# Hybrid decoder block on one core: stores issued from GpSimd's queue in place of SyncE's

## The chip, the cores and the metric

The kernel runs on one core of one Trainium2 chip. The metric is device time in microseconds (us), the median of three runs: 1451.16 (1450.82 to 1451.53). The core's engines are TensorE (PE), VectorE (DVE), ScalarE (ACT), GpSimd (POOL) and SyncE (SP); each runs its own list of instructions in order, and semaphores order the lists against each other.

## The reference

One decoder block in fp32 over x of 1024 tokens and 1024 channels (D), with a feed-forward width of 2816. Norms and small steps are cut.

```python
h = rms_norm(x, norm_mix_g)
rnn_x, rnn_gate, sgu_u, sgu_v, gate_a, gate_b = split(h @ w_in)          # six of 1024 columns
rnn_x = causal_depthwise_conv(rnn_x, conv_w, conv_b)                     # width 4
y_a = gelu(rnn_gate) * rg_lru(rnn_x, ...)                                # gates, then a linear scan over time
y_b = chunked_sgu(gelu(sgu_u), gelu(sgu_v), ...)                         # u * (tril(W) LN(v) + b), chunks of 128
merged = sigmoid(gate_a) * (y_a @ w_proj_a) + sigmoid(gate_b) * (y_b @ w_proj_b)
x = x + merged @ w_out
h = rms_norm(x, norm_ffn_g)
g, u = split(h @ w_gate_up)
x = x + (silu(g) * u) @ w_down
return rms_norm(x, norm_final_g)
```

## The kernel before

Every fp32 operand of a large product is split into a high and a low part, and one product is three matmuls (L97 to L99): high by high, high by low, low by high. ACT makes the high part (L93), DVE the low part (L94). The matrix products run as Strassen-Winograd: a pair of output columns is seven products M1 to M7 on blocks and sums of blocks (`wino`), whose results DVE and ACT combine out of PSUM (L231 to L249: L236, L243 and L246 on DVE, L233, L239 and L241 on ACT). The order inside a pair is M1, M5, M6, M2, M7, M3, M4; some instructions end up in another place because the scheduler orders each engine's list.

The stages are: norm and transposes; SGU's v; then pairs of r (RG-LRU), u (SGU) and g (both merge gates) in the order of `IN`; projection b; projection a with the merge; output projection with residual; eleven pairs of the gated feed-forward; the down projection.

What one stage makes for a later one goes through DRAM. `store(dst, src)` (L724) writes it, `load` (L721) reads it back. `store` has five uses: `y_store` writes the blocks and block sums of the branch outputs to ya_d and yb_d (names of tiles: u_y, u_m, u_u, mix, yb_sd, yb_s for branch b, gg, ya_sd, ya_s for branch a); `gate_pair` writes the sigmoids to sga_d and sgb_d (tiles g_y, g_m, g_u, sg); `to_mb` writes projection b's gated result to mb_d (tiles pb_y, pb_m, pb_u, sb); `norm2` writes the residual to x2_d; `ff_outs` writes the feed-forward operands and their sums, made on GpSimd (L1147 to L1150), to ffa_d and ffs_d. All loads, the weights (wraw, L133) and the stores of the final output (L1240) are issued by SP as well, and SP does its instructions in order: a store whose data are not made yet holds what stands behind it.

The buffers that the text speaks of: ya_s and yb_s share two buffers (tag "s4"), written by DVE at L760 or in the sums below it; the staged loads (yb_r.., ya_r.., mrg, x2, ff) share the six buffers of `stg` (STG = 6); a gate of projection b is loaded one or two steps ahead into a tile sb. The program is built with `dynamic_dma_scratch_size=256` (L1350), the space in SBUF kept for descriptors of DMAs issued by GpSimd; the kernel before issues none.

Of the kernel before, what the change touches and what calls it, by code (L numbers as in the profile page):

```python
# [51 lines left out]
def block_kernel(ctx: ExitStack, tc: tile.TileContext, a: dict, out: bass.AP):  # L52
    nc = tc.nc
    act, dve, pool, pe = nc.scalar, nc.vector, nc.gpsimd, nc.tensor
# [667 lines left out]
        nc.sync.dma_start(dst, src)  # L722

    def store(dst, src):  # L724
        nc.sync.dma_start(dst, src)

    ms.__exit__(None, None, None)
    new_misc("misc1")
    with tc.tile_pool(name="phr", bufs=2) as wk:
# [12 lines left out]
        def y_store(d, name, f, h, y):  # L742


            k = f % 4
            n = "A12" if f >= 4 else "A11"
            if h == 0:
                store(d[n][:, k], y)
            elif f >= 4:
                store(d["A22"][:, k], y)  # L750
            else:
                store(d["sd"][:, k, 1], y)
            other = halves.pop((name, f, 1 - h), None)
            if other is None:
                halves[name, f, h] = y
                return
            y0, y1 = (y, other) if h == 0 else (other, y)
            s, r = halves.pop((name, f))
            if f < 4:
                dve.tensor_sub(s, y0, y1)  # L760
                store(d["sd"][:, k, 0], s)
                return
            dve.tensor_sub(r[:, 0], y1, r[:, 0])
            dve.tensor_add(r[:, 1], r[:, 1], y1)
            dve.tensor_sub(s, y0, r[:, 0])
            store(d["S2"][:, k], r[:, 0])
            store(d["S1"][:, k], r[:, 1])
            store(d["S4"][:, k], s)
# [591 lines left out]
```

## Time and profile before

| | |
|---|---|
| median of three runs | 1451.16 us (1450.82 to 1451.53) |
| profiled execution | 1452.88 us |
| its span, first to last instruction | 1451.2 us |
| granted TensorE clock, mean | 0.99 |
| busy: PE, DVE, ACT, POOL | 1400.2, 1098.3, 793.5, 74.8 us |

All durations come from the profiled execution. A line number is that of the kernel. In a time line each row is the start in us, the length in us, the engine, the line, the operation and what it writes and reads; a bracket at the end is the idle time of the engine ahead of it and what ended it. A DMA's row is its issue; when it has landed is a separate figure. PE's share of 96% means that what counts is where PE is not busy, and which other engine or transfer stands on the way at that moment.

### The profile page before, as it was taken

The numbers are of one execution on the slowest core, as the hardware profiler recorded it, in microseconds if no ns is written. First come the engines' busy times: TensorE is split into PE (matmuls) and PEld (weight loads), VectorE is DVE, ScalarE is ACT, GpSimd is POOL, SyncE is SP. The second block draws the span as 40 slices with busy tenths as digits, with TensorE's granted clock in tenths as the row PEclk, the third lists the DMA queues.
The fourth block names the chain that finished last, engine by engine and source line by source line (L and its number), as shares of the span: only waits on it lengthen the run. The fifth ranks groups of instructions, "written<-read, shape, count | busy, mean of one in ns | idle before, by whom it ended". The sixth has DMA issues, their size and how long they took to land.

```text
span 1451.2 us, 17181 instructions
## 1 busy us (share of the span) xinstructions
PE 1400.2 (96%) x6192; PEld 1153.3 (79%) x6192; DVE 1098.3 (76%) x1803; ACT 793.5 (55%) x1315; POOL 74.8 (5%) x59
## 2 busy tenths in 40 slices
PE   7998699999999999999999999999999999999997
PEld 5776587788888888778888788888888888888886
DVE  6878889988888878597855966666666665697585
ACT  6456668789888876262443633333333333444454
POOL 0000000000000000000000011111111111100000
PEclk9998899999999999999999999999999999999999
DMA  8412445632233367676531032222222226853342
GB/s 294 157 44 70 157 173 176 206 123 93 78 122 140 117 261 293 234 263 217 188 122 44 22 134 109 109 109 110 105 88 105 103 81 266 312 196 109 109 138 80
DMA packets 72821, 212.45 MB, mean 146 GB/s; under 512 B 6560, under 2 KB 20384, under 8 KB 60192
## 3 DMA queue, kind: packets, MB, share of 16 engines
q1 hardware_dynamic: 72592, 211.32, 40.8%
q8 instruction: 48, 0.79, 0.2%
q14 instruction: 37, 0.30, 0.1%
q10 hardware_dynamic: 144, 0.04, 0.0%
HBM read 148.68 MB, written 62.65 MB: 146 GB/s over the span
## 4 chain that ended last, share of the span: by engine, by line
PE 76%; DVE 11%; ACT 6%; DMA 4%; issue 2%; SPq 0%; DVEq 0%; ACTq 0%; POOL 0%; POOLq 0%
PE f_p L99 10%; PE f_p L97 10%; PE f_p L98 10%; PE d_M L98 5%; PE d_M L97 5%; PE d_M L99 5%; PE g_p L99 3%; PE g_p L98 3%; PE g_p L97 3%; PE r_p L99 2%; DMA sb<-sgb_d 2%; PE r_p L98 2%; PE r_p L97 2%; PE po L97 2%; PE po L99 2%; PE po L98 2%
## 5 line engine op out<-in xcount | busy, mean ns | idle before, releaser
L93 ACT ACTIVATE dl_M<-wraw 128x512 fp32r<-128x512 f32 x77 | 48.6, 631 | 104.8 <-PE d_M L99 89.8
L98 PE MATMUL d_M<-d_M,dl_M 128*128 128x512 f32 x264 | 102.8, 389 | 0.0
L97 PE MATMUL d_M<-d_M,dl_M 128*128 128x512 f32 x264 | 102.7, 389 | 0.0
L99 PE MATMUL d_M<-d_M,dl_M 128*128 128x512 f32 x264 | 102.7, 389 | 0.0
L93 ACT ACTIVATE f_t<-wraw 128x512 fp32r<-128x512 f32 x88 | 55.5, 630 | 83.8 <-PE f_p L99 71.4
L94 DVE TENSOR_TENSOR dl_M<-wraw,dl_M 128x512 fp32r<-128x512 f32 x77 | 54.0, 701 | 51.5 <-ACT dl_M L93 51.3
L94 DVE TENSOR_TENSOR f_t<-wraw,f_t 128x512 fp32r<-128x512 f32 x88 | 71.7, 815 | 23.7 <-ACT f_t L93 22.6
L97 PE MATMUL f_p<-m,f_b 128*128 128x512 f32 x176 | 69.2, 393 | 0.0
L98 PE MATMUL f_p<-m,f_b 128*128 128x512 f32 x176 | 69.0, 392 | 0.0
L99 PE MATMUL f_p<-m,f_b 128*128 128x512 f32 x176 | 69.0, 392 | 0.0
L98 PE MATMUL f_p<-m,f_t 128*128 128x512 f32 x176 | 68.5, 389 | 0.0
L99 PE MATMUL f_p<-f_S,f_t 128*128 128x512 f32 x176 | 68.5, 389 | 0.0
L97 PE MATMUL f_p<-f_S,f_t 128*128 128x512 f32 x176 | 68.5, 389 | 0.0
L99 PE MATMUL f_p<-m,f_t 128*128 128x512 f32 x176 | 68.5, 389 | 0.0
L97 PE MATMUL f_p<-m,f_t 128*128 128x512 f32 x176 | 68.5, 389 | 0.0
L98 PE MATMUL f_p<-f_S,f_t 128*128 128x512 f32 x176 | 68.5, 389 | 0.0
L93 ACT ACTIVATE f_b<-wraw 128x512 fp32r<-128x512 f32 x66 | 41.1, 626 | 36.8 <-PE f_p L99 31.6
L94 DVE TENSOR_TENSOR f_b<-wraw,f_b 128x512 fp32r<-128x512 f32 x66 | 45.3, 687 | 19.6 <-ACT f_b L93 18.9
L97 PE MATMUL pv<-wv,h 128*128 128x512 f32 x128 | 51.5, 403 | 7.8 <-ACT wv L93 7.8
L97 PEld LDWEIGHTS d_M<-d_M,dl_M 128*128 128x128 f32 x264 | 49.6, 188 | 10.4
L98 PEld LDWEIGHTS d_M<-d_M,dl_M 128*128 128x128 f32 x264 | 49.6, 188 | 10.3 <-DVE d_M L94 0.2
L99 PEld LDWEIGHTS d_M<-d_M,dl_M 128*128 128x128 f32 x264 | 49.6, 188 | 10.3
(504 smaller groups left out, 4213.0 us busy)
## 6 DMA issues: line engine op xcount, KB each, us to landing
wraw<-in_w_gu_dram SPq DMA_DIRECT2D x22, 1024.0 KB, 4.8
wd<-in_w_down_dram SPq DMA_DIRECT2D x11, 1024.0 KB, 9.4
wraw<-in_w_r_dram SPq DMA_DIRECT2D x8, 1024.0 KB, 6.1
wraw<-in_w_g_dram SPq DMA_DIRECT2D x8, 1024.0 KB, 4.8
wraw<-ffs_d SPq DMA_DIRECT2D x8, 1024.0 KB, 5.1
wraw<-ffa_d SPq DMA_DIRECT2D x6, 1024.0 KB, 6.1
xn<-in_x_dram SPq DMA_DIRECT2D x8, 512.0 KB, 6.2
wraw<-in_w_u_dram SPq DMA_DIRECT2D x4, 1024.0 KB, 5.3
```

Of the source, the lines that this page charges most:

```text
L93: act.activation(hi, src, AF.Copy)
L94: (eng or dve).tensor_sub(lo, src, hi.bitcast(F32))
L97: pe.matmul(o, lh, rh, start=start, stop=False, **kw)
L98: pe.matmul(o, lh, rl, start=False, stop=False, **kw)
L99: pe.matmul(o, ll, rh, start=False, stop=stop, **kw)
```

## The change

`store` issues its DMA from GpSimd (`pool`) in place of SP. Loads, weights, the spatial mix and the final output stay on SP.

```diff
--- before.py
+++ after.py
@@ -722,7 +722,7 @@
         nc.sync.dma_start(dst, src)
 
     def store(dst, src):
-        nc.sync.dma_start(dst, src)
+        pool.dma_start(dst, src)
 
     ms.__exit__(None, None, None)
     new_misc("misc1")
```

138 stores move. SP's list goes from 377 rows to 238, GpSimd's from 64 to 202. The other engines keep their work; some rows change places, because the scheduler sees other queues.

The first place is the burst of stores in which pair u2 ends while r0 makes its output. SP before (a load of mix and one of graw stand between the stores; the brackets name the semaphores that the row waits for, DMAHW those of DMAs from SP):

```order
L725 DMA yb_d_A_80<-u_y_1887 128x512 [waits DMAHW7_49,DVE_49]
L722 DMA mix_2060<-mix_d_108 128x512 [waits DMAHW4_49,DMAHW0_49]
L725 DMA yb_d_A_81<-u_m_1908 128x512 [waits DMAHW1_49,DVE_49]
L725 DMA ya_d_A_72<-gg_1723 128x512 [waits DMAHW2_49,DVE_49]
L725 DMA yb_d_S_83<-yb_sd_1996 128x512 [waits DMAHW3_49,DVE_49]
L725 DMA yb_d_S_82<-yb_sd_1996 128x512 [waits DVE_49]
L722 DMA graw_2074<-in_rg_w_dram 128x256 [waits DMAHW5_49,DVE_49]
L725 DMA yb_d_A_80<-u_u_1925 128x512 [waits DMAHW6_49,DVE_49]
L725 DMA yb_d_S_84<-yb_s_1995 128x512 [waits DMAHW7_49,DVE_49]
```

GpSimd after (DMASW are the semaphores of DMAs from GpSimd):

```order
L725 DMA yb_d_A_80<-u_y_1887 128x512 [waits DMASW4_49,DVE_49]
L725 DMA yb_d_A_81<-u_m_1908 128x512 [waits DMASW5_49,DVE_49]
L725 DMA ya_d_A_72<-gg_1723 128x512 [waits DMASW6_49,DVE_49]
L725 DMA yb_d_S_83<-yb_sd_1996 128x512 [waits DMAHW6_49,DMASW7_49,DVE_49]
L725 DMA yb_d_S_82<-yb_sd_1996 128x512 [waits DMASW0_49,DVE_49]
L725 DMA yb_d_A_80<-u_u_1925 128x512 [waits DMASW1_49,DVE_49]
L725 DMA yb_d_S_84<-yb_s_1995 128x512 [waits DMASW2_49,DVE_49]
```

The stores stand alone on GpSimd's list, in the same order, and each waits for its semaphore's use eight stores earlier.

The second place is the start of the loads of projection b's operands (yb_r..). SP before:

```order
L725 DMA ya_d_A_74<-gg_4128 128x512 [waits DMAHW1_49,DVE_49]
L725 DMA ya_d_S_76<-ya_sd_4410 128x512 [waits DMAHW2_49,DVE_49]
L725 DMA ya_d_S_75<-ya_sd_4410 128x512 [waits DMAHW3_49,DVE_49]
L725 DMA ya_d_S_77<-ya_s_4409 128x512 [waits DMAHW4_49,DVE_49]
L133 DMA wraw_4509<-in_w_pb_dram 128x2048 [waits DMAHW5_49,DVE_49]
L722 DMA yb_rA_4464<-yb_d_A_79 128x2048 [waits DMAHW3_49,DMAHW2_49,DMAHW4_49,DMAHW1_49,DMAHW6_49,PE_49,Pool_49]
L722 DMA yb_rS_4466<-yb_d_S_82 128x2048 [waits DMAHW7_49]
L722 DMA yb_rS_4468<-yb_d_S_83 128x2048 [waits DMAHW0_49]
L722 DMA yb_rA_4470<-yb_d_A_80 128x2048
```

SP after:

```order
L133 DMA wraw_4312<-in_w_g_dram 128x2048 [waits DMAHW2_49,DVE_49]
L133 DMA wraw_4509<-in_w_pb_dram 128x2048 [waits DMAHW5_49,DMAHW3_49,DVE_49]
L722 DMA yb_rA_4464<-yb_d_A_79 128x2048 [waits DMASW5_49,DMASW4_49,DMASW6_49,DMASW3_49,DMASW7_49,DMASW2_49,DMAHW1_49,DMASW1_49,DMAHW7_49,PE_49,Pool_49]
L722 DMA yb_rS_4466<-yb_d_S_82 128x2048
L722 DMA yb_rS_4468<-yb_d_S_83 128x2048
L722 DMA yb_rA_4470<-yb_d_A_80 128x2048
L722 DMA yb_rS_4472<-yb_d_sd 128x4x512
L722 DMA yb_rS_4474<-yb_d_S_84 128x2048
L133 DMA wraw_4644<-in_w_pb_dram 128x2048 [waits DMAHW4_49,DVE_49]
```

The four gate weights stand directly ahead of the loads, and the first load waits for seven semaphores of GpSimd's queue; wraw_4644 stands behind six loads. ACT, which splits what is loaded there (yb_A, yb_S) and empties g7's PSUM banks (g_m, g_u), before:

```order
L93 ACTIVATE yb_A_4637<-yb_rA_4464 128x2x512 x2
L239 ACTIVATE g_m_4659<-g_p_4646 128x512
L93 ACTIVATE yb_S_4682<-yb_rS_4466 128x2x512 x2
L93 ACTIVATE yb_S_4722<-yb_rS_4468 128x2x512 x2
L93 ACTIVATE yb_A_4773<-yb_rA_4470 128x2x512 x2
L835 ACTIVATE g_y_4635<-g_y_4635 128x512
L241 ACTIVATE g_u_4680<-g_p_4622 128x512
```

ACT after:

```order
L93 ACTIVATE yb_A_4637<-yb_rA_4464 128x2x512 x2
L239 ACTIVATE g_m_4659<-g_p_4646 128x512
L93 ACTIVATE yb_S_4682<-yb_rS_4466 128x2x512 x2
L241 ACTIVATE g_u_4680<-g_p_4622 128x512
L93 ACTIVATE yb_S_4722<-yb_rS_4468 128x2x512 x2
```

L241 moved two splits ahead, and PE's 12 matmuls of g7's M7, which write g_p_4622 after it, moved ahead of those of M3.

The third place is projection b's first half, where sb are the gates that it loads. SP before:

```order
L725 DMA mb_d_86<-pb_y_4818 128x512 [waits DMAHW6_49,DVE_49]
L722 DMA sb_4942<-sgb_d_99 128x512 [waits DMAHW7_49,DMAHW4_49]
L722 DMA ya_rS_5077<-ya_d_sd 128x4x512 [waits DMAHW0_49]
L725 DMA mb_d_88<-pb_m_4839 128x512 [waits DMAHW1_49,DVE_49]
L722 DMA sb_4965<-sgb_d_101 128x512 [waits DMAHW7_49,DMAHW2_49]
L722 DMA ya_rS_5079<-ya_d_S_77 128x2048 [waits DMAHW3_49]
L725 DMA mb_d_88<-pb_m_4859 128x512 [waits DVE_49]
L722 DMA sb_4985<-sgb_d_99 128x512 [waits DMAHW5_49,DMAHW2_49]
L722 DMA sb_5081<-sgb_d_102 128x512 [waits DMAHW6_49]
L722 DMA sb_5083<-sgb_d_103 128x512
```

SP after:

```order
L722 DMA ya_rS_5077<-ya_d_sd 128x4x512 [waits DMAHW3_49,DVE_49,Activation_49]
L722 DMA ya_rS_5079<-ya_d_S_77 128x2048 [waits DMAHW5_49,DVE_49,Activation_49]
L133 DMA wraw_4924<-in_w_pb_dram 128x2048 [waits DMAHW4_49,DVE_49]
L133 DMA wraw_4948<-in_w_pb_dram 128x2048 [waits DVE_49]
L722 DMA sb_4916<-sgb_d_100 128x512 [waits DMAHW6_49,DVE_49]
L722 DMA sb_5081<-sgb_d_102 128x512 [waits DMASW2_49,DMAHW7_49,DMASW1_49,DMASW0_49]
L722 DMA sb_4942<-sgb_d_99 128x512 [waits DMAHW6_49,DMAHW0_49,DVE_49]
L722 DMA sb_5083<-sgb_d_103 128x512 [waits DMAHW1_49,DMASW3_49,DMASW1_49]
L722 DMA sb_4965<-sgb_d_101 128x512 [waits DMAHW2_49,DMAHW0_49,DVE_49]
L722 DMA sb_4985<-sgb_d_99 128x512 [waits DMAHW3_49,DMAHW2_49,DVE_49]
L722 DMA sb_5007<-sgb_d_101 128x512 [waits DMAHW4_49,DMAHW3_49,DVE_49]
```

The loads of sb follow each other with no store between, and the two large loads of ya_rS stand ahead of all of them.

## Rows read from the trace of the kernel before

**Rows 1.** The page's head and busy times, whole span.
```profile
span 1451.2 us, 17181 instructions
...
PE 1400.2 (96%) x6192; PEld 1153.3 (79%) x6192; DVE 1098.3 (76%) x1803; ACT 793.5 (55%) x1315; POOL 74.8 (5%) x59
```

**Rows 2.** Stretches of 25 us: busy time, granted clock, DMA share, GB/s.
```profile
225.00:250.00 25.00, 24.24 (x107) 19.65 (x106) 24.96 (x42) 18.24 (x28) 0.00 (x0) 1.00 0.67 227
275.00:300.00 25.00, 23.52 (x103) 18.71 (x102) 24.64 (x40) 17.11 (x27) 0.10 (x1) 1.00 0.60 204
525.00:550.00 25.00, 25.00 (x112) 20.71 (x111) 19.82 (x26) 16.79 (x24) 0.00 (x0) 1.00 1.00 387
600.00:625.00 25.00, 21.57 (x94) 17.15 (x94) 18.42 (x27) 9.32 (x14) 0.00 (x0) 1.00 0.68 219
625.00:650.00 25.00, 23.43 (x102) 18.80 (x101) 22.08 (x30) 19.02 (x27) 0.00 (x0) 1.00 0.69 243
```

**Rows 3.** PE's waits, 170 to 1440 us: total, times, longest.
```profile
PE pb_p L97 <- ACT pb_u L241: 2.9, 2, 1.6
PE pb_p L97 <- DVE pb_m L243: 2.1, 1, 2.1
```

**Rows 4.** Source line L725: one group of stores, and landing times of all.
```profile
L725 SPq DMA_DIRECT2D sga_d<-g_y x8: 319/326/332, 309.6 to 549.7; - x8
...
DMA to landing us min/median/max: 2.0/2.6/16.8
```

**Rows 5.** GpSimd's groups by form: one of the FF sums.
```profile
L1148 POOL TENSOR_TENSOR ff3s<-ff3a 128x512 f32<-128x512 f32 x1 | 1.7, 1679 | 14.0 <-DVE ff3a L1159 14.0
```

**Rows 6.** Time line of SP, the two bursts: start, length, instruction.
```profile
222.78 0.32 SPq L725 DMA_DIRECT2D yb_d_A<-u_y  x1
...
239.64 0.32 SPq L725 DMA_DIRECT2D ya_d_sd<-ya_s  x1
...
264.86 0.32 SPq L725 DMA_DIRECT2D yb_d_A<-u_y  x1
...
268.78 0.32 SPq L725 DMA_DIRECT2D yb_d_A<-u_m  x1
...
271.19 0.32 SPq L725 DMA_DIRECT2D yb_d_S<-yb_s  x1
```

**Rows 7.** Time line of DVE, near the ends of the bursts.
```profile
238.94 0.68 DVE L760 TENSOR_TENSOR ya_s<-gg 128x512 f32<-128x512 f32 x1
...
281.93 0.69 DVE L760 TENSOR_TENSOR ya_s<-gg 128x512 f32<-128x512 f32 x1
```

**Rows 8.** Time line of SP, ahead of projection b's operand loads.
```profile
516.27 0.33 SPq L725 DMA_DIRECT2D sga_d<-g_y  x1
...
523.96 0.32 SPq L725 DMA_DIRECT2D ya_d_S<-ya_s  x1
...
527.10 0.32 SPq L722 DMA_DIRECT2D yb_rA<-yb_d_A  x1
```

**Rows 9.** ACT's and PE's time lines there, and landing times of yb_rA.
```profile
539.52 2.00 ACT L93 ACTIVATE yb_A<-yb_rA 128x1024 fp32r<-128x1024 f32 x2
...
549.62 0.58 ACT L241 ACTIVATE g_u<-g_p 128x512 f32<-128x512 f32 x1
...
546.98 0.39 PE L97 MATMUL g_p<-h_S,g_b 128*128 128x512 f32 x1
...
DMA to landing us min/median/max: 6.5/11.6/12.7
```

**Rows 10.** Tile sb: idle before its use, landing; PE's time line, waits in brackets.
```profile
  DMA sb<-sgb_d: 14.9, 7
...
DMA to landing us min/median/max: 2.1/4.6/8.4
...
605.67 0.50 PE L97 MATMUL pb_p<-yb_S,pb_t 128*128 128x512 f32 x1 [1.36 <-ACT pb_u L241]
...
613.51 0.50 PE L97 MATMUL pb_p<-yb_A,pb_t 128*128 128x512 f32 x1 [2.06 <-DVE pb_m L243]
```

## The prediction, made before the run

> **What bounds the kernel now.** I read the busy shares first [rows 1]: TensorE (PE) works 1400.2 of 1451.2 us, so at most 51 us are open at all. Next the stretches [rows 2]. A stretch of 25 us shows 25.00 of PE where nothing is lost. In the stretches shown PE loses 0.76 at 225:250, 1.48 at 275:300, nothing at 525:550, 3.43 at 600:625 and 1.57 at 625:650. Then PE's own waits from 170 to 1440 us [rows 3]: for pb_p (projection b) they are 2.9 and 2.1 us. So the change can win some 5 us in projection b and little elsewhere, and it loses wherever a store that lands later holds DVE, ACT or a load long enough to stop an engine that is full. The reader is to see that DVE is as full as PE in 225:250, with 24.96 of 25.00 us.
>
> **What one moved store costs.** The trace of before has no DMA on GpSimd's queue, so its price is bounded. On SP an issue took 0.32 us [rows 6], and the stores landed 2.0 to 16.8 us after issue, 2.6 in the median [rows 4]. The low end: the queue holds a store for its issue alone, 0.32 us, and the next may leave at once. The high end: the median landing plus one GpSimd pass over a 128x512 tile, 1.68 us [rows 5], as a stand-in for writing the descriptors in software, 4.3 us. Let s be the time for which one store holds the queue before the next is on its way. I take s = 2.9, the median landing plus the issue (2.6 + 0.32), because the kernel gives GpSimd's descriptors only 256 bytes (L1350), and a store of 128 rows of 2 KB fills most of so little. I expect one store in flight at a time.
>
> [...]
>
> **Term 1, the first burst (222.8 to 239.6).** Thirteen stores are issued here in 16.9 us [rows 6]; on the new queue they need 13 x 2.9 = 37.7 us. The seventh, yb_d_S_84<-yb_s_1995, lands at 222.8 + 7 x 2.9 = 243.1. Its source is one of two buffers of the tag s4, and DVE's L760 writes that buffer next (ya_s_2010), before at 238.94 [rows 7]. DVE is thus held 4.2 us. Behind it in DVE's order stand the weight sums and splits of u3 (L207, L94), the combination that releases PE's bank (L236) and the convolution that xs and the gate matmuls (pgt) wait for. DVE has 0.04 us free there and PE already lost 0.76, so nothing covers it: +4.2.
>
> **Term 2, the next burst (264.9 to 282.6).** The same pattern with less in front: stores leave SP at 264.86, 268.78 and then within 2.4 us up to the sixth at 271.19 [rows 6]. At s = 2.9 the first is through by 267.8, and five follow from 268.8 on: 268.8 + 5 x 2.9 = 283.3. DVE's L760 wrote that buffer at 281.93 [rows 7]: +1.4. Later each RNN and gate pair makes 9 stores, 26 us of queue, and the pairs come 34 us apart (8 stores of g_y from 309.6 to 549.7 [rows 4]): nothing.
>
> **Term 3, the loads of projection b's operands.** yb_rA and the five loads behind it were issued at 527.10 [rows 8], when space came free. In the changed order the first of them waits for seven of the eight semaphores of GpSimd's queue. Eight stores stand there between 516.27 and 523.96 [rows 8], and all must land: 516.3 + 8 x 2.9 = 539.5. The first load took 6.5 us then [rows 9], so the data are there at 546.0, where ACT began on them at 539.52 [rows 9]. ACT takes its instructions in order: the split of yb_A (2.0), g_m (0.6), yb_S (2.0), g_u of L241 (0.6), so L241 ends at 546.0 + 5.2 = 551.2. The changed order puts g7's M7, 12 matmuls into the bank that L241 empties, ahead of M3, so at the place where M3 began, 546.98 [rows 9]. PE waits 4.2 us. For wraw_4644, now behind six loads of 1 MB, I add 0.6, a guess between 0 and 3: +4.8. The cover is PE's own work up to 547; had M7 stayed behind M3, M3 would be cover too.
>
> **Term 4, projection b's gate loads.** SP no longer blocks in front of each sb load on a store that waits for DVE (rows of SP in the order below), and two loads of 1 MB, ya_rS, that stood between sb loads now stand ahead of them. DVE waited 14.9 us for sb in 7 places, on loads that took 4.6 us in the median [rows 10], and PE lost 1.36 and 2.06 us in this chain [rows 10] and 1.57 in the next 25 us [rows 2], together 5.0. I count 4.0 of it back: -4.0. Not all, because the last of these also hangs on ACT's weights for projection a, and wraw_5246 there comes to stand behind two loads that wait for stores. If these run late, a store's hold of 2.9 comes off the gain.
>
> **At nothing.** The issue time saved on SP (138 x 0.32 us) lies on a queue with idle time. GpSimd's own sums in the FF stage, 4 x 1.7 us per pair [rows 5], now share a queue with the two stores behind them; three pairs of buffers (STG = 6) leave two whole pairs of time. The x2 stores have no reader before the down projection. If the cover in FF were gone, each of 11 pairs could cost one store, 2.9.
>
> **Sum.** +4.2 + 1.4 + 4.8 - 4.0 = +6.4 us. The profiled execution took 1452.88 us, so 1459.3 for a profiled run; the median of the three runs lies 1.72 lower, at 1451.16, and there the sum gives 1457.6.
>
> **Rivals.**
> - *Stores overlap, or s is 2.2 or less.* Then the bursts cost nothing: the seventh store lands by 222.8 + 15.4 = 238.2, ahead of 238.94 [rows 7]; the barrier opens by 516.3 + 17.6 = 533.9, and the data are there at 540.4, 0.9 after ACT's start, which ACT's gaps take up. Term 4 alone remains: 1447.2. For it speak the low landing times of 2.0 [rows 4]; against it only the small descriptor space. [...]
> - *The terms cancel, s about 2.5.* Term 1 is 240.3 - 238.9 = 1.4, term 2 zero, term 3 (516.3 + 20.0 + 6.5 + 5.2 - 547.0 = 1.0, and 0.6) 1.6, term 4 -4.0: -1.0, so 1450, and no change up to s = 2.7. For it speaks the DMA share of only 0.60 in 275:300 [rows 2].
> - *A store holds the queue for 3.5 us or more.* This is my forecast's mechanism with another outcome, and it decides from there on. At 4.0: 222.8 + 28 - 238.9 = 11.9; 268.8 + 20 - 281.9 = 6.9; 516.3 + 32 + 6.5 + 5.2 - 547.0 + 0.6 = 13.6; -4.0. Sum +28, so 1480; at 4.3 it is 1486. For it speak the landings of up to 16.8 under load [rows 4] and the DMA share of 0.67 in the first burst [rows 2]. [...]
> - *No change through no effect* would need the waits on the new semaphores to fall where nothing is due; the order shows them in front of yb_rA, so I give this nothing of its own.
>
> **How the numbers follow.** The three runs lie 0.7 us apart, so 0.2%, 2.9 us, tells a change from none. Forecast (s 2.7 to 3.4, 1453 to 1467): 0.42. Overlap, 1447: 0.20. Cancel, 1450 to 1453: 0.18. Long hold, 1467 to 1486: 0.20. Faster is the overlap and a tenth of the cancelling case: 0.22. Same is the rest of that case and the edge of the forecast: 0.18. Slower: 0.60. The sum moves by some 20 us per us of s. The range reaches down to the overlap case, 1446.5, and up to s = 3.8, 1475; the forecast's own range is 1453 to 1467.
>
> **What would show it.** Right: a store row on GpSimd's queue with 2 to 4 us from one issue to the next in the bursts; DVE's L760 waiting for a yb_d_S DMA by some 4 us near 239; the yb_rA loads issued near 539 and a PE wait on g_u's L241 near 547; DVE's waits for sb well below 14.9. Wrong: issues a fraction of a us apart, or yb_rA issued near 527 as before. Waits of DVE in the FF stage on ffs or ffa, or of PE on wraw<-in_w_pa, would mean that a step counted at nothing was the one that mattered.

## The result, and the profile after

The changed kernel took 1497.34 us in the median (1491.88 to 1498.07, 4 runs), 1.0301 times the time before (95% interval 1.028 to 1.0323). Forecast were 1457.6 and a range up to 1475: the direction was right, the size too small by a factor of seven. The trace counts 142 stores on the new queue (POOL's x201 against x59), four more than the 138 named above.

The head of the page after, with its busy times and the new queue (packets, MB, share of 16 engines):

```profile
span 1496.3 us, 17260 instructions
...
PE 1414.1 (95%) x6192; PEld 1162.7 (78%) x6192; DVE 1102.3 (74%) x1803; ACT 793.9 (53%) x1315; POOL 150.0 (10%) x201
...
q0 software_dynamic: 13280, 53.75, 9.1%
```

Against [rows 1] the span is 45.1 us longer. PE's idle time went from 51.0 to 82.2 us, so 31.2 of it are waits. The other 13.9 are in PE's busy time, 1414.1 in place of 1400.2 for the same 6192 matmuls: after the waits they ran at a lower clock (between 140 and 1400 us 84 matmuls start at the lower level, a granted clock of 0.50, and 20 before).

The time of the same matmul in both traces shows where it went (an offset of 0.5 us stands from the start on):

| same matmul of PE | before | after | later by | gained or lost since the row above |
|---|---|---|---|---|
| u_p, before the first stores tell | 175.0 | 175.6 | 0.5 | |
| r_p, behind the stores of the first two u pairs (165 to 190) | 200.1 | 212.2 | 12.1 | +11.6 |
| u_p, behind the burst of term 1 | 250.1 | 271.4 | 21.3 | +9.2 |
| pgt, behind the burst of term 2 | 300.2 | 327.2 | 27.1 | +5.7 |
| g_p, end of the gate pairs | 537.7 | 564.8 | 27.1 | 0.0 |
| pb_p, behind the operand loads of term 3 | 562.7 | 598.3 | 35.6 | +8.5 |
| pb_p, middle of projection b | 600.1 | 636.6 | 36.5 | +0.9 |
| pa_p, start of projection a | 637.6 | 680.2 | 42.6 | +6.1 |
| pa_p, third pair of projection a | 712.6 | 757.7 | 45.1 | +2.5 |
| d_M, near the end | 1437.6 | 1482.7 | 45.0 | 0.0 |

The stretches where it was lost (us busy of PE, PEld, DVE, ACT, POOL with counts, then granted clock, DMA share, GB/s):

```profile
200.00:225.00 25.00, 18.15 (x72) 14.82 (x73) 18.17 (x35) 15.11 (x24) 2.30 (x5) 0.86 0.47 158
250.00:275.00 25.00, 17.77 (x66) 14.12 (x65) 16.51 (x27) 13.12 (x20) 3.95 (x8) 0.80 0.56 178
300.00:325.00 25.00, 19.47 (x78) 15.56 (x77) 19.28 (x31) 14.35 (x23) 3.96 (x8) 0.86 0.41 146
575.00:600.00 25.00, 20.33 (x77) 16.61 (x78) 19.45 (x22) 19.19 (x27) 2.19 (x4) 0.86 1.02 422
650.00:675.00 25.00, 19.92 (x79) 15.91 (x78) 18.82 (x27) 12.20 (x17) 2.75 (x5) 0.86 0.60 200
```

[Rows 2] had 24.24 in the first burst's stretch and 25.00 at 525:550; here 18.15, 17.77, 19.47, 20.33 and 19.92, and the clock is 0.80 or 0.86 in each. PE's waits answer to [rows 3] (total, times, longest):

```profile
PE r_p L97 <- DVE r_m L243: 12.8, 2, 7.2
...
PE r_p L97 <- ACT r_u L241: 8.1, 1, 8.1
PE g_p L97 <- ACT g_u L241: 5.4, 1, 5.4
PE pb_p L97 <- DVE pb_m L243: 5.1, 1, 5.1
```

Before, r_p waited 0.6 us for DVE's L243 and not at all for ACT's L241, nor did g_p.

GpSimd's queue in the two bursts at 165 to 213 and 235 to 274 us (start, length, instruction, idle time before):

```profile
190.14 0.54 POOL L725 DMA_DIRECT2D yb_d_sd<-u_m  x1 [2.05 <-issue]
192.73 0.55 POOL L725 DMA_DIRECT2D yb_d_sd<-mix  x1 [2.06 <-DVE r_t L94]
200.94 0.56 POOL L725 DMA_DIRECT2D yb_d_sd<-yb_s  x1 [7.65 <-issue]
...
244.16 0.55 POOL L725 DMA_DIRECT2D yb_d_S<-yb_sd  x1 [2.15 <-DVE r_t L94]
246.79 0.55 POOL L725 DMA_DIRECT2D yb_d_S<-yb_sd  x1 [2.08 <-DVE yb_s L765]
249.41 0.55 POOL L725 DMA_DIRECT2D yb_d_A<-u_u  x1 [2.08 <-DVE xc L908]
256.20 0.54 POOL L725 DMA_DIRECT2D yb_d_S<-yb_s  x1 [6.24 <-issue]
258.85 0.55 POOL L725 DMA_DIRECT2D yb_d_A<-mix  x1 [2.10 <-issue]
```

Most of these stores leave 2.6 us apart (2.59 to 2.65): 0.55 of issue, and some 2.06 in which the queue waits. A store lands 2.3 us after its issue there, and the next leaves 0.3 us later; in the whole trace none leaves before the one ahead of it has landed. Two distances are far longer, 8.2 us (192.73 to 200.94) and 6.8 (249.41 to 256.20). SP's time line has a 1 MB weight load beside each of them, and, third, the first operand load of projection b:

```profile
192.72 0.33 SPq L133 DMA_DIRECT2D wraw<-in_w_r_dram  x1
...
250.05 0.38 SPq L133 DMA_DIRECT2D wraw<-in_w_r_dram  x1
...
568.57 0.33 SPq L722 DMA_DIRECT2D yb_rA<-yb_d_A  x1
```

DVE's L760, the writer of the two s4 buffers, with what it waited for in brackets; [rows 7] have it at 238.94 and 281.93 with no wait:

```profile
203.27 0.69 DVE L760 TENSOR_TENSOR yb_s<-u_y,mix 128x512 f32<-128x512 f32 x1 [9.90 <-DMA yb_d_sd<-yb_s]
...
258.64 0.69 DVE L760 TENSOR_TENSOR ya_s<-gg 128x512 f32<-128x512 f32 x1 [7.49 <-DMA yb_d_S<-yb_s]
...
308.13 0.69 DVE L760 TENSOR_TENSOR ya_s<-gg 128x512 f32<-128x512 f32 x1 [4.79 <-DMA yb_d_S<-yb_s]
```

PE behind the first of these waits. The matmuls start 0.42 to 0.43 us apart up to 210.0 and 0.23 to 0.24 apart from 210.4 on, the lower and the higher level of the clock:

```profile
206.85 0.79 PE L97 MATMUL r_p<-h_S,r_t 128*128 128x512 f32 x1 [8.09 <-ACT r_u L241]
...
209.15 0.63 PE L99 MATMUL r_p<-h_S,r_t 128*128 128x512 f32 x1
209.57 0.63 PE L97 MATMUL r_p<-h_S,r_t 128*128 128x512 f32 x1
...
210.62 0.40 PE L97 MATMUL r_p<-h_S,r_t 128*128 128x512 f32 x1
210.85 0.40 PE L98 MATMUL r_p<-h_S,r_t 128*128 128x512 f32 x1
```

The granted clock of that stretch is the third figure from the end (columns as in the stretches above):

```profile
204.00:210.00 6.00, 3.15 (x8) 2.48 (x8) 5.10 (x15) 3.27 (x6) 0.64 (x2) 0.50 0.58 154
```

The engine stood still for 8.09 us, and its granted clock was 0.50 from 204 to 210; from 210.4 to 212 it was 1.00.

At the start of projection b, ACT (compare [rows 9]):

```profile
574.08 2.00 ACT L93 ACTIVATE yb_A<-yb_rA 128x1024 fp32r<-128x1024 f32 x2 [7.36 <-DMA yb_rA<-yb_d_A]
...
579.04 0.58 ACT L241 ACTIVATE g_u<-g_p 128x512 f32<-128x512 f32 x1
```

The eight stores left from 543.75 on and the last landed at 568.4, just before SP issues the load above; ACT waits 7.36 for it, and PE 5.42 for g_u.

### The profile page after: what moved, and what is told of

Same layout as the page of the kernel before. It is cut to its first block, busy times and chain, and to the rows that moved or that the text cites. A ratio compares the mean times of both kernels' runs of the same rounds, so it can differ in the third digit from the quotient of the medians.

```text
span 1496.3 us, 17260 instructions
## 1 busy us (share of the span) xinstructions
PE 1414.1 (95%) x6192; PEld 1162.7 (78%) x6192; DVE 1102.3 (74%) x1803; ACT 793.9 (53%) x1315; POOL 150.0 (10%) x201
## 4 chain that ended last, share of the span: by engine, by line
PE 66%; DVE 11%; issue 10%; DMA 6%; ACT 5%; POOL 1%; SPq 0%; POOLq 0%; ACTq 0%; DVEq 0%
PE f_p L99 9%; PE f_p L98 9%; PE f_p L97 9%; PE d_M L98 4%; PE d_M L97 4%; PE d_M L99 4%; PE g_p L99 3%; PE g_p L98 3%; PE g_p L97 3%; PE r_p L97 2%; PE r_p L98 2%; PE r_p L99 2%; PE po L99 2%; PE po L98 2%; PE po L97 2%
```

## The experiments

Each was timed against the kernel before on the same chip; that took 1452.6 to 1452.9 in the median there.

**Is it the room for GpSimd's descriptors?** Two kernels with the same instruction lists on every engine, only the size differs:

```diff
-    nc = _bacc.Bacc("TRN2", target_bir_lowering=False, num_devices=1, dynamic_dma_scratch_size=256)
+    nc = _bacc.Bacc("TRN2", target_bir_lowering=False, num_devices=1, dynamic_dma_scratch_size=320)
```

Theory R is that the room holds one store at a time: the next one goes out when the one before has landed. How many stores 320 bytes hold no run had shown; if it is two, R puts this kernel at 1452 to 1465 us.

> The same instruction lists as the changed kernel; only the room for GpSimd's descriptors is 320 bytes in place of 256. [...] Theory W (GpSimd itself needs 2.6 us to write a store's descriptors, or waits for DVE to do so): the distance stays 2.6, and the time 1497. Theory O (the loss comes from the new order of the lists, SP's loads behind stores): also 1490 or more, with or without shorter distances.

Measured: 1461.97 us, ratio 1.0058 (1.0037 to 1.0078), within R's range.

> As ring320 with 512 bytes, room for three stores. R: distance near 1 us or less, the bursts hold nobody, and what is left is the order of the lists: 1446 to 1453 us. W and O: 1497 as with 256 bytes.

Measured: 1460.06 us, ratio 1.0047 (1.0031 to 1.0064), 7 us above R's range. The burst of term 1 on GpSimd's queue in ring512:

```profile
226.79 0.54 POOL L725 DMA_DIRECT2D yb_d_A<-u_m  x1 [1.18 <-DVE u_m L791]
227.39 0.55 POOL L725 DMA_DIRECT2D ya_d_A<-gg  x1
228.59 0.54 POOL L725 DMA_DIRECT2D yb_d_S<-yb_sd  x1 [0.65 <-DVE yb_sd L763]
...
231.66 0.55 POOL L725 DMA_DIRECT2D yb_d_A<-u_u  x1 [1.32 <-DVE u_u L791]
```

Issues now stand 0.60 and 1.2 us apart, what the data allow. At most one store of this queue is in flight in the trace with 256 bytes, two with 320 (in ring320 the stores of 230.03 and 230.89, for one) and three with 512 (226.79, 227.39 and 228.59); none lands in less than 2.3 us in either. By the ratios 37 of the 44 us go with 256 bytes more, and in ring512's trace all but 1.1 us of what was lost in the three bursts. Theory W (writing the descriptors takes the time) falls, since the writing is the same. Of the two sizes 320 gives nearly all. The time left over, 0.5%, is more than R alone allowed: so part of O may be true as well.

**What holds the queue, by itself.** The kernel before with stores that nobody reads:

```diff
+    def probe(first, n, width):
+        for i in range(first, first + n):
+            pool.dma_start(probe_d[i][:, :width], g_fin[:, 0, :width])
+    later(2 * KD + 6, lambda: probe(0, 16, HALF))
+    later(2 * KD + 16, lambda: probe(16, 8, P))
+    later(2 * KD + 24, lambda: probe(24, 8, D))
```

> The kernel before with 32 more stores from GpSimd in the down projection, where it has nothing else to do: 16 of 128x512 (256 KB), 8 of 128x128 (64 KB), 8 of 128x1024 (512 KB), all of one constant tile, back to back, none read again; 256 bytes. R (one store in the room at a time): distances of 2.6 us in quiet stretches, near 2.2 for 64 KB and 3.2 for 512 KB, and 5 to 8 us where a 1 MB load of SP runs at the same time. W (GpSimd's writing of descriptors sets it): the same distance for all three sizes and loads, since each has 128 rows. The time is no more than 1 us above before in either case.

The sizes follow each other (16, 8 and 8; the 17th leaves at 1344.61). GpSimd's time line, two pairs of 256 KB, then one of 64 KB, then one of 512 KB:

```profile
1292.24 0.54 POOL L1218 DMA_DIRECT2D probe_d<-g_fin  x1 [6.65 <-issue]
1294.84 0.55 POOL L1218 DMA_DIRECT2D probe_d<-g_fin  x1 [2.06 <-issue]
1300.60 0.54 POOL L1218 DMA_DIRECT2D probe_d<-g_fin  x1 [5.21 <-issue]
1303.18 0.55 POOL L1218 DMA_DIRECT2D probe_d<-g_fin  x1 [2.04 <-issue]
...
1351.19 0.54 POOL L1218 DMA_DIRECT2D probe_d<-g_fin  x1 [1.66 <-issue]
1353.38 0.55 POOL L1218 DMA_DIRECT2D probe_d<-g_fin  x1 [1.65 <-issue]
...
1380.90 0.54 POOL L1218 DMA_DIRECT2D probe_d<-g_fin  x1 [5.27 <-issue]
1384.11 0.54 POOL L1218 DMA_DIRECT2D probe_d<-g_fin  x1 [2.67 <-issue]
```

The distance is 2.6 us for 256 KB, 2.2 for 64 KB and 3.2 for 512 KB, and 5.8 where a load of 1 MB came between (SP issued one at 1294.27); the first of all took 8.0. Of the first three stores the median landing is 6.9 us, and from the second to the third it is 7.2: here, too, the next leaves 0.3 us after the landing. So the distance follows the transfer and its neighbours, not the work of writing, which is 128 rows in each. The time of this kernel was 1453.03 in its single run, as before.

**Which stores cost?** All others go from SP, with 256 bytes.

> Only the branch outputs (ya_d, yb_d) are stored from GpSimd, with 256 bytes; gates, merge, residual and feed-forward operands go from SP as before. R: the three bursts keep their loss (11.6, 9.2 and 5.7 us by the comparison of the two traces), the start of projection b loses less since four stores fewer stand there, projection b is as before: 1476 to 1484 us. O: if the wait of SP's loads at projection b were the main part, 1460 or less.

Measured: 1488.66 us, ratio 1.0249 (1.0228 to 1.027), 5 us above what I expected. The wait of PE for g_u at the start of projection b was 8.4 in its trace, more than the 5.4 with the gates in the queue too. Yet the loads of projection b's operands left sooner, at 560.02 in place of 568.57, and ACT waited less for them. What ACT waited for, in only_y and then in the changed kernel (total, times, longest):

```profile
ACT g_u L241 <- DMA sga_d<-g_y: 5.9, 1, 5.9
...
ACT yb_A L93 <- DMA yb_rA<-yb_d_A: 2.0, 2, 1.5
```

```profile
ACT yb_A L93 <- DMA yb_rA<-yb_d_A: 8.5, 2, 7.4
```

In only_y the gate store sga_d<-g_y is issued on SP at 563.41 behind the six loads and lands 18.0 us later; ACT's L241 is held by it. So the four stores fewer did shorten the wait for the loads, and a store that stayed on SP cost more than that.

> The changed kernel with 256 bytes, but the 12 stores of the first two u pairs (165 to 190 us), which the prediction had not priced, stay on SP. The comparison of the traces puts 11.6 us on them: 1484 to 1488. If the loss were only passed on to the next burst (DVE late anyway), 1493 to 1498.

Measured: 1488.61 us, ratio 1.0247 (1.0218 to 1.0276), just above what I expected: by the ratios 7.8 us of the changed kernel's time come from the 12 stores that I had not priced. In its trace the 11.6 us of the first burst are gone, but projection a loses 5.5 us in place of 2.5.

> Only the residual's and the feed-forward operands' stores (30) go from GpSimd, with 256 bytes. I priced them at nothing: no change, 1449 to 1454. If a store held GpSimd's sums long enough to stop DVE at the buffers of stg, each of 11 pairs could cost one hold of 2.9: up to 1480.

Measured: 1452.72 us, ratio 0.9998 (0.9986 to 1.0009). This step stands.

> Only the 16 stores of mb_d are issued from GpSimd, with 256 bytes. My prediction's term 4 says 4 us faster, 1447. The traces of the two kernels say that projection b lost 6 us in the changed kernel: if that comes from these stores alone, 1455 to 1458; if it was left over from what came before (late operands, late gates), 1447 to 1452.

Measured: 1459.48 us, ratio 1.0047 (1.0031 to 1.0063). The 16 stores lose in a stage where I had them gain 4 us.

**Why projection b loses.** The change of queue also changed DVE's order. These are its rows for the last two gate products of the first two pairs (sb) and the next pair's first combinations, before:

```
L985 TENSOR_TENSOR sb_5031<-sb_5031,pb_p_4785 128x512 [waits DMAHW4_49]
L236 TENSOR_TENSOR pb_y_5098<-pb_y_5098,pb_p_5143 128x512 [waits DMAHW1_49,PE_49]
L243 TENSOR_TENSOR pb_m_5119<-pb_m_5119,pb_p_5085 128x512 [waits PE_49]
L985 TENSOR_TENSOR sb_5050<-sb_5050,pb_p_4805 128x512 [waits DMAHW6_49,DMAHW0_49]
```

and after (in only_mb the same):

```
L985 TENSOR_TENSOR sb_5031<-sb_5031,pb_p_4785 128x512 [waits DMAHW6_49]
L985 TENSOR_TENSOR sb_5050<-sb_5050,pb_p_4805 128x512 [waits DMAHW7_49,DMASW6_49]
L236 TENSOR_TENSOR pb_y_5098<-pb_y_5098,pb_p_5143 128x512 [waits DMASW2_49,PE_49]
L243 TENSOR_TENSOR pb_m_5119<-pb_m_5119,pb_p_5085 128x512 [waits DMASW3_49,PE_49]
```

The product sb_5050 waits for a gate load into the one buffer that sb_5031 has in use until its own store has landed. It now stands ahead of L243, which empties the bank that PE waits for. Tying it behind L243 keeps the queue and undoes this; in the traces of ring512 and ring512_order nothing else changes place but one store and one load (an excerpt of the edit):

```diff
+                if (which, h, f) == ("b", 1, 2):
+                    held.append((g, product))
+                    return
+                if (which, h, f) == ("b", 1, 5):
+                    g2, last = held.pop()
+                    dve.scalar_tensor_tensor(g2[:, :1], c[:, :1], 0.0, g2[:, :1], ALU.mult, ALU.add)
+                    last()
                 product()
```

> ring512, and in projection b the product of the last gate of the first two pairs (sb_5050) is tied behind DVE's L243 (pb_m_5117) by an operation on one column that adds zero, so that DVE's order there is again nearly that of the kernel before. Theory S (what is left of the loss in projection b is that this product, which waits for a gate load and that for a store's landing, was moved ahead of the release of PE's bank): the 4.0 us at this place and the 2.2 behind it go, 1451 to 1455. Theory Q (GpSimd's longer way from issue to landing delays the gates whatever the order): 1459 to 1461 as ring512.

Measured: 1456.03 us, ratio 1.0027 (1.0017 to 1.0036), 1 us above S's range and 3 below Q's. PE's wait at this place in ring512, and in ring512_order:

```profile
PE pb_p L97 <- DVE pb_m L243: 6.1, 1, 6.1
```

```profile
PE pb_p L97 <- DVE pb_m L243: 2.0, 1, 2.0
```

4.1 us less there; 2.9 by the ratios of the two kernels. The comparison of the traces leaves 4.5 us: 1.5 in the first burst, 2.1 behind the operand loads (563 to 575), the rest mostly at the end of projection b.

> Only the 16 stores of mb_d go from GpSimd, with 512 bytes and the same tie. S: my term 4 gets its chance, 1447 to 1452 (only_mb had 1459). Q: 1456 to 1459.

Measured: 1450.94 us, ratio 0.9981 (0.9967 to 0.9995), just below the kernel before. PE's waits in projection b; [rows 3] had 2.9 and 2.1:

```profile
PE pb_p L97 <- ACT pb_u L241: 1.6, 1, 1.6
...
PE pb_p L97 <- DVE pb_m L243: 0.4, 1, 0.4
```

Waits as small as these also change from one execution to the next: probe and only_x2_ff have the order of the kernel before through all of projection b, and there the two waits were 1.3 and 2.2, and 4.4 and 0.5. What tells here is the time, not one wait; the 6.1 above lies outside that spread.

> Control for mb512_order: the kernel before, all stores on SP, with the tie of sb_5050 behind L243 alone. If mb512_order's gain came from the queue (its trace is 3.3 us ahead at 613 us and 2.2 at the end), this one stays at 1451 to 1454. If the tie alone makes it, 1448 to 1450.

Measured: 1453.29 us, ratio 1.0004 (0.9993 to 1.0015). So the tie alone brings no gain. It isn't a clean control: with the stores on SP the tie moved other rows of DVE, ACT and PE too. Whether mb512_order's gain comes from the queue or from the order that came with it is not shown.

> mb512_order with 256 bytes: one store at a time in projection b, DVE's order tied. The stores of mb there come 4 to 8 us apart, so the room should cost little except where a store stands beside a 1 MB load: R gives 1452 to 1456, 1 to 5 above mb512_order; if the order was all of only_mb's loss, the same as mb512_order, 1450 to 1452.

Measured: 1458.9 us, ratio 1.0041 (1.0025 to 1.0058), by the ratios 8.7 us above the same lists with 512 bytes, and 3 above what I expected. The profiled execution took 1455.04, 4 more than that of mb512_order, and one wait of PE carries it (mb512_order has 1.6 in its place):

```profile
PE pb_p L97 <- ACT pb_u L241: 6.0, 1, 6.0
```

Ahead of it ACT stood 3.3 us for the landing of a store of pb_m and 1.3 for one of pb_u, which it doesn't in mb512_order. In projection b, too, the room is the larger part, not the order alone as only_mb had let me think: only_mb, which is mb256_order without the tie, is only 0.9 us slower by the ratios, which is within the noise.

> 512 bytes; all stores from GpSimd except mb_d. The bursts cost nothing with this room, projection b's list is as before; left is the start of projection b (SP's loads behind GpSimd's stores, L241 and M7 moved): 3 to 4 us in ring512_order's trace, so 1454 to 1457. If that place were harmless in itself, 1451 to 1453.

Measured: 1456.79 us, ratio 1.0026 (1.0014 to 1.0038). The time came as expected, the place did not: by the matmuls of the two traces 4.0 us are lost in the first burst, which has room for three stores here, and only 1.9 behind the operand loads. What of the 1.3 to 2.1 behind the operand loads in the kernels with 512 bytes belongs to the stores' landing, to L241 and M7, or to SP's weight behind six loads, I did not separate.

The first burst lost 1.1, 1.5 and 4.0 us in ring512, ring512_order and all_but_mb_512. In each it is one wait of PE for u_m, of 1.1, 1.6 and 2.4 us, and ahead of it DVE waits for a load of mix that SP issued. In all_but_mb_512:

```profile
183.53 0.75 DVE L791 SCALAR_TENSOR_TENSOR mix<-mix,pv,sh 128x512 f32<-128x512 f32 x1 [1.88 <-DMA mix<-mix_d]
...
185.53 0.50 PE L97 MATMUL u_p<-h_A,u_t 128*128 128x512 f32 x1 [2.45 <-DVE u_m L243]
```

DVE's wait was 1.54 in ring512 and 0.34 in the kernel before. In all_but_mb_512 alone the granted clock was 0.50 behind it (186.5 to 189.5), which makes up most of the rest of the 4.0. So this loss is not the room's; why that load landed later is open.

## Why the prediction was wrong, by its steps

*One store in flight at a time* was right, and shown by 256 against 320 and 512 bytes with the same lists. That a store fills most of 256 bytes had no row behind it; one, two and three in flight with 256, 320 and 512 bytes put a store at over 128 and at most 160 bytes, an estimate. The room is the cause of 37 of the 44 us.

*The size of s* was wrong in kind. I took one number, 2.9. It is 2.6 in most places of the bursts and up to 8.2 beside a 1 MB load. In the kernel before, such a store merely landed late ([rows 4] run up to 16.8), and in the whole trace a store's landing held another engine once (ACT's L241, 2.4 us); with room for one it held all behind it, 8.2 us from 192.73 on. In term 1 the seventh store landed at 258.5, 23.3 us after the first, so s was 3.3, and DVE's L760 waited 7.49 in place of 4.2; with the clock behind it 9.2 us were lost. Term 2: 4.79 in place of 1.4, and 5.7 lost. But at s = 3.3 the sum of the prediction gives only +14.4, 1465.6: the size of s alone doesn't explain the miss.

*Where the sum began* was, by the traces, the largest error in one piece. "The first burst (222.8 to 239.6)" is not the first: 12 stores stand at 165 to 190, with the same two s4 buffers behind them. DVE waited 2.58 and 9.90 there, PE 8.09, and 11.6 us were lost (7.8 by first_burst_on_sp) where the sum had nothing. I had begun PE's waits at 170 and had read a stretch without losses as one that cannot lose.

*The clock* had no term. Behind each of PE's five new waits of 5 to 8 us, and behind one of 2.8, the matmuls ran at the lower level, and PE's busy time grew by 13.9 us, nearly a third of the loss. Even correct waits would have left the sum short by that.

*Term 3*: the operand loads waited as forecast, PE 5.42 in place of 4.2; with the lower clock behind it 8.5 in place of 4.8.

*Term 4* had the wrong sign: +6.1 in place of -4.0. Its sign of being right, waits of DVE for sb well below 14.9, did not appear either:

```profile
  DMA sb<-sgb_d: 13.1, 7
```

A gain was seen only in mb512_order, 0.19%, with room for more than one store and with the tie. I read SP's list in the order of the changed kernel and not DVE's, and took loads that could leave earlier as products that come earlier.

*At nothing*: right for the residual and the feed-forward stage (only_x2_ff). Projection a was not priced at all and lost 2.5; no run shows why.

The rival of a long hold came nearest, with 1480 at s = 4.0 and 1486 at 4.3. Its reason, the landings under load, was right, but that it came near is in part luck: s was 3.3 in term 1 and 3.1 over the eight stores of term 3, not 4.0, and it, too, lacked the first burst and the clock and kept term 4's gain.

## What to carry to other kernels

Before a DMA is moved to GpSimd's queue, look how many bytes are set aside for its descriptors: with room for one store (here 256 bytes), the queue was as slow as each landing, 2.6 us in most places, and a late one, up to 8.2, delayed all behind it. When a queue gets slower, price every burst on it, quiet ones too, and add the matmuls at the lower clock behind the long waits of PE (13.9 us here, behind waits of 2.8 to 8.1). When a scheduler orders the lists, read every engine's list at the place of each term, not only that of the engine that was changed.

## What the runs showed of the hardware

With 256 bytes of descriptor room a store from GpSimd occupied the queue until it had landed, and the next left 0.3 us behind that at the soonest (2.3 and 2.6 us after the issue in the changed kernel). It was 2.2 us from one to the next for 64 KB, 2.6 for 256 KB, 3.2 for 512 KB (probe). Beside a 1 MB load of SP 256 KB took 5.6 to 8.0 us in probe and up to 8.2 in the changed kernel. With 320 and 512 bytes two and three stores were in flight at once (ring320, ring512). After 8.09 us without work PE's matmuls started 0.43 us apart, at a granted clock of 0.50, before they went back to 0.23, at 1.00 (changed kernel, 206.85 to 212).
